# Attention in fp16 on one core: the columns of ones beside the values, written by VectorE and no longer by GpSimd

## The chip, the core and the metric

The kernel runs on one core of a Trainium2 chip. A core has five engines with instruction queues of their own: TensorE (PE in the profile; its weight loads are PEld), VectorE (DVE), ScalarE (ACT), GpSimd (POOL) and SyncE (SP), which here only issues DMAs. Engines wait for each other on semaphores. The metric is the device time of one execution in microseconds; the kernel before has a median of 124.57 us over seven runs.

## The reference

Plain softmax attention over 8 batches of 8 heads, with 512 positions of 64 elements, in float32:

```python
scores = np.einsum('bhqd,bhkd->bhqk', q, k) / np.sqrt(64)
attn = np.exp(scores - scores.max(axis=-1, keepdims=True))
attn = attn / attn.sum(axis=-1, keepdims=True)
out = np.einsum('bhqk,bhkd->bhqd', attn, v)
```

## The kernel before, in words

The 64 heads are worked on in 32 pairs (`NP`), numbered g. A tile of a pair holds both heads: 128 partitions, and 4 rows of 64 elements for each head in each partition.

For a pair, SyncE loads k, q and v (`load`, L318; six buffers for each). GpSimd casts them from float32 to fp16 (`cast_qk`, L331, and `cast_v`, L323). TensorE transposes q and k against an identity matrix (`transposes`, L348), VectorE copies the transposes out of PSUM (`copy`, L355), and TensorE makes the scores transposed, keys in the partitions and queries along the free axis (`scores`, L374). ScalarE takes the exponential of 1024 columns at a time (L379); the maximum is not subtracted. For six of the groups of scores VectorE computes the exponential itself, in seven instructions (L393 to L428). Then TensorE multiplies the exponentials by the values (`values`, L462), and VectorE divides by the sum (`normalise`, L440 and L441). SyncE stores the result (L449).

The sums of the softmax come out of the same matmul as the result. Twelve tiles (`vps`, `NV = 12`) hold the cast values of a pair: for each of the 2 x 4 blocks, 64 columns of values and one more column that holds 1.0. So a value matmul has 65 columns, and the last of them is the sum of the exponentials. The tiles are used in turn, g modulo 12. The columns of ones are written once, before anything else uses the tiles (L608); the casts of v write only the 64 columns beside them. Each write is a memset of 128 partitions and 8 elements, one in every 65.

The order of the work on each engine is fixed when the program is built. The opening is written out by hand: the first loads (`first_loads`, L505 on ScalarE's queue for k and L506 on SyncE's for q, a head at a time), the loads of the next pairs, the identity matrix (`make_identity`, two operations on GpSimd), the ones, and then `first_pair`. In `first_pair` TensorE multiplies a constant by itself (`busy`, L510) until the first q and k are there. VectorE, ScalarE and GpSimd cast parts of the first pair (L520 to L525), TensorE transposes them (L539, L545), VectorE copies them out (L567 to L591), and the first exponentials follow (L557). After the opening the class `Plan` sets the order, with a model of the three busy engines that steps through the kernel 5 ns at a time when the program is built. Nothing in it refers to the ones.

Of the kernel before, what the change touches and what calls it, by code (L numbers as in the profile page):

```python
# [229 lines left out]
def kernel(  # L230
# [7 lines left out]
    nc = tc.nc  # L238
    B, H, S, D = q.shape
# [38 lines left out]
    vps = [cpool.tile([P, 2, NI, D + 1], FP16, name=f"vp{n}") for n in range(NV)]  # L278
# [29 lines left out]
    def load(g, names):  # L308
        if g >= NP:
            return  # L310
        for name in names:
            src = {"q": q, "k": k, "v": v}[name]
            t = load_tile(g, name)
            if name == "v" and g in HALVED:
                for h in range(2):
                    nc.sync.dma_start(out=t[:, h], in_=source(src, g)[:, h])
                continue
            nc.sync.dma_start(out=t[:, :, :, :], in_=source(src, g))  # L318

    def cast_v(g):  # L320
        if g >= NP:
            return
        nc.gpsimd.tensor_copy(out=vps[g % NV][:, :, :, 0:D], in_=raw[g]["v"][:, :, :, :])  # L323

    def cast_qk(g):
        if g >= NP:
            return
        t = qpool.tile([P, 2, NI, P], FP16, tag="qkp", name=f"qkp_{g}")
        for n, name in ((1, "k"), (0, "q")):
            eng = nc.vector if (g, name) == (1, "q") else nc.gpsimd  # L330
            eng.tensor_copy(  # L331
                out=t[:, n].rearrange("p i (h d) -> p h i d", h=2),
                in_=raw[g][name][:, :, :, :],
            )
        qkp[g] = t

    def feed(g):
        load(g + 5, "kqv")
        cast_qk(g + 3)
        cast_v(g + 2)  # L340
# [9 lines left out]
    def copy(g):  # L350
        if g == 1:
            for n in (1, 0):
                nc.vector.tensor_copy(out=tqk[g][:, n], in_=tps[g][:, n].rearrange("p i c -> p (i c)"))  # L353
            return
        nc.vector.tensor_copy(  # L355
            out=tqk[g][:, :, :], in_=tps.pop(g).rearrange("p n i c -> p n (i c)")
        )
# [79 lines left out]
    def normalise(u, n):  # L437
        o, x = os[u // 7], u % 7
        rc = opool.tile([P, 7, 1], FP32, tag="rc", name=f"rc_{u}")
        nc.vector.reciprocal(out=rc[:, 0:n], in_=o[:, x : x + n, D : D + 1])  # L440
        nc.vector.tensor_tensor(  # L441
            out=ring[:, u % NU : u % NU + n, :],
            in0=o[:, x : x + n, 0:D],
            in1=rc[:, 0:n].broadcast_to([P, n, D]),
            op=AluOp.mult,
        )
        while heads and heads[0][2] + NI <= u + n:
            g, h, u0 = heads.pop(0)
            nc.sync.dma_start(  # L449
                out=source(out, g)[:, h], in_=ring[:, u0 % NU : u0 % NU + NI, :]  # L450
            )
# [49 lines left out]
    def first_loads():  # L501
        tk = load_tile(0, "k")
        tq = load_tile(0, "q")
        for h in range(2):
            nc.scalar.dma_start(out=tk[:, h], in_=source(k, 0)[:, h])  # L505
            nc.sync.dma_start(out=tq[:, h], in_=source(q, 0)[:, h])  # L506
# [91 lines left out]
    with tc.manual_schedule():  # L598
        first_loads()
        load(1, "kq")  # L600
        load(0, "v")
        for g in range(2, 5):
            load(g, "kq")
            load(g - 1, "v")
        load(4, "v")
        make_identity(nc, ident)
        for n in range(NV):
            nc.gpsimd.memset(vps[n][:, :, :, D : D + 1], 1.0)  # L608
        first_pair()
        cast_qk(1)  # L610
        cast_v(0)
        cast_qk(2)
        cast_v(1)
        feed(0)
        do = {
            "transposes": transposes,
            "scores": scores,
            "values": values,
            "feed": feed,
            "raise": raise_,  # L620
            "copy": lambda g, b: copy(g),
            "pass": pass_,
            "norm": lambda u, n, b: normalise(u, n),
        }
        for what, *args in Plan(groups, NP, 3).run():
            do[what](*args)
# [30 lines left out]
```

## Time and profile before

| | |
|---|---|
| runs | 124.23, 124.46, 124.47, 124.57, 125.81, 125.82, 125.86 us; median 124.57 |
| the profiled execution | 124.47 us |
| its span, first to last instruction | 122.7 us |
| granted TensorE clock | 0.996 of full speed |
| busy: ScalarE, TensorE, VectorE, GpSimd | 114.3, 108.3, 99.4, 76.5 us |
| the 12 memsets of ones on GpSimd | first start 1.24 us, 138 ns each, 0.53 us together |
| first instruction of VectorE | 3.21 us |

The span is what the profile covers; the execution is 1.77 us longer. Busy time counts an engine's own instructions, not its waits, and the engines work beside each other, so their busy times add up to more than the span. A line of the timeline gives the start, the duration, the engine, the line of the kernel, the operation, and its tiles; the brackets behind it hold how long the engine stood idle before, and what released it.

### The profile page before, as it was taken

The page shows a single profiled execution, that of the slowest core. Times are in us where ns is not written, and L with a number is a line of the kernel's source. Part 1 is how long each engine was busy: PE and PEld are TensorE (multiplying, and loading weights), DVE is VectorE, ACT ScalarE, POOL GpSimd, SP SyncE. Part 2 cuts the span into 40 slices and gives each one's busy share as a digit, 9 for nine tenths or more (in the row PEclk, how much of TensorE's full clock was granted, in tenths as well). Part 3 has the DMA queues.
Part 4 walks back from the last instruction along what each step waited for, and adds up shares of the span by engine and source line. Part 5 has one row for each costly group of instructions (what it writes and reads, how often), then busy time and mean ns, then how long its engine had stood idle before and what let it go on. Part 6 is the DMA issues. An engine that isn't in the chain of part 4 may idle for free.

```text
span 122.7 us, 3967 instructions
## 1 busy us (share of the span) xinstructions
PE 108.3 (88%) x1565; PEld 67.5 (55%) x1565; DVE 99.4 (81%) x159; ACT 114.3 (93%) x127; POOL 76.5 (62%) x113
## 2 busy tenths in 40 slices
PE   7979788989898898998999997989999998899950
PEld 2546445647465465765456573656655665567540
DVE  0546999999989998699999899896979898875260
ACT  4499999999999999999999999999999999999940
POOL 3269799997988579295666958185956679000000
PEclk9999999999999999999999999999999999999998
DMA  3999999999999999995989999997999993131342
GB/s 119 292 352 384 384 377 382 379 353 284 366 352 333 292 331 344 318 330 204 260 275 285 280 308 316 287 305 236 300 293 335 342 326 132 48 115 59 129 138 83
DMA packets 35603, 33.82 MB, mean 276 GB/s; under 512 B 2688, under 2 KB 35584, under 8 KB 35584
## 3 DMA queue, kind: packets, MB, share of 16 engines
q1 hardware_dynamic: 35152, 33.24, 82.8%
q10 hardware_dynamic: 432, 0.33, 0.8%
q8 instruction: 12, 0.20, 0.7%
q14 instruction: 7, 0.06, 0.1%
HBM read 25.17 MB, written 8.39 MB: 273 GB/s over the span
## 4 chain that ended last, share of the span: by engine, by line
ACT 49%; PE 27%; issue 18%; DVE 2%; ACTq 0%
ACT pt L379 49%; PE st L374 10%; PE o L462 8%; PE tp L348 3%; PE st_0a L510 2%; DVE tqk L353 1%; PE st L550 1%; PE o_last L477 1%; DVE ring L441 1%; PE tp_qb L545 0%; DVE obl L490 0%; PE tp_qa L545 0%; PE st L545 0%; PE st_0a L550 0%; DVE kt L591 0%
## 5 line engine op out<-in xcount | busy, mean ns | idle before, releaser
L379 ACT ACTIVATE pt<-st 128x1024 f16<-128x1024 f32 (+1 forms) x120 | 109.4, 1327 | 0.1
L374 PE MATMUL st<-tqk 64*128 64x512 f16 x248 | 48.1, 384 | 7.6 <-ACT pt L379 6.6
L462 PE MATMUL o<-vp,pt 128*128 128x65 f16 x1008 | 46.9, 195 | 1.3 <-ACT pt L379 0.9
L462 PEld LDWEIGHTS <-pt 128*128 128x128 f16 x1008 | 37.1, 98 | 18.4 <-issue 14.7
L331 POOL CAST qkp<-k 128x512 f16<-128x512 f32 x31 | 21.2, 683 | 24.0 <-DMA k<-in_k_dram 15.6
L323 POOL CAST vp<-v 128x512 f16<-128x512 f32 x32 | 29.9, 935 | 0.9 <-DMA v<-in_v_dram 0.8
L331 POOL CAST qkp<-q 128x512 f16<-128x512 f32 x30 | 26.6, 887 | 0.6 <-DMA q<-in_q_dram 0.4
L374 PEld LDWEIGHTS <-tqk 64*128 64x128 f16 x248 | 13.2, 93 | 21.1 <-issue 12.4
L441 DVE TENSOR_TENSOR ring<-o,rc 128x448 f32<-128x448 f32 (+2 forms) x37 | 22.6, 612 | 1.3
L355 DVE COPY tqk<-tp 128x1024 f16<-128x1024 f16 x30 | 20.6, 685 | 2.4 <-PE tp L348 2.1
L348 PE MATMUL tp<-ident,qkp 128*128 128x128 f16 x248 | 19.5, 220 | 0.0
L348 PEld LDWEIGHTS <-qkp 128*128 128x128 f16 x248 | 14.0, 98 | 6.9 <-issue 4.8
L428 DVE SCALAR_TENSOR_TENSOR y<-y,m 128x1024 f32<-128x1024 f32 x12 | 16.4, 1365 | 0.0
L440 DVE RECIPROCAL rc<-o 128x7 f32<-128x7 f32 (+2 forms) x37 | 7.3, 198 | 9.3 <-PE o L462 9.3
L428 DVE SCALAR_TENSOR_TENSOR pt<-y,e 128x1024 f16<-128x1024 f32 x6 | 8.1, 1348 | 0.0
L428 DVE SCALAR_TENSOR_TENSOR y<-m 128x1024 f32<-128x1024 f32 x6 | 8.1, 1346 | 0.0
L393 DVE TENSOR_SCALAR z<-st 128x1024 uint32<-128x1024 f32 x6 | 7.3, 1221 | 0.5 <-PE st L374 0.4
L417 DVE TENSOR_SCALAR e<-z 128x1024 uint32<-128x1024 uint32 x6 | 6.1, 1022 | 0.0
L406 DVE TENSOR_SCALAR m<-z 128x1024 uint32<-128x1024 uint32 x6 | 5.2, 867 | 0.0
L510 PE MATMUL st_0a<-const-bfloat16-1.0 128*128 128x512 bf16 (+1 forms) x8 | 2.9, 548 | 0.8 <-PEq L641 0.8
L510 PEld LDWEIGHTS <-const-bfloat16-1.0 128*128 128x128 bf16 x15 | 1.6, 120 | 2.6 <-issue 2.4
L520 DVE CAST q<-q 128x128 f16<-128x128 f32 x1 | 0.2, 227 | 3.2 <-DMA q<-in_q_dram 3.2
(43 smaller groups left out, 18.9 us busy)
## 6 DMA issues: line engine op xcount, KB each, us to landing
out_dram<-ring SPq DMA_DIRECT2D x63, 128.0 KB, 3.6
k<-in_k_dram SPq DMA_DIRECT2D x31, 256.0 KB, 4.7
q<-in_q_dram SPq DMA_DIRECT2D x31, 256.0 KB, 4.8
v<-in_v_dram SPq DMA_DIRECT2D x27, 256.0 KB, 5.0
v<-in_v_dram SPq DMA_DIRECT2D x10, 128.0 KB, 4.7
k<-in_k_dram ACTq DMA_DIRECT2D x2, 128.0 KB, 2.8
q<-in_q_dram SPq DMA_DIRECT2D x2, 128.0 KB, 2.5
out_dram<-obl SPq DMA_DIRECT2D x1, 64.0 KB, 2.7
```

The source lines that it names most:

```text
L323: nc.gpsimd.tensor_copy(out=vps[g % NV][:, :, :, 0:D], in_=raw[g]["v"][:, :, :, :])
L331: eng.tensor_copy(out=t[:, n].rearrange("p i (h d) -> p h i d", h=2), in_=raw[g][name][:, :, :, :],)
L348: nc.tensor.transpose(tps[g][:, n, i, :], qkp[g][:, n, i, :], ident)
L355: nc.vector.tensor_copy(out=tqk[g][:, :, :], in_=tps.pop(g).rearrange("p n i c -> p n (i c)"))
L374: nc.tensor.matmul(st[:, x, :], kc, qc, start=True, stop=True)
L379: nc.scalar.activation(out=pt[:, 0:size, :], in_=st[:, 0:size, :], func=EXP, scale=scale)
L393: nc.vector.tensor_scalar(out=r["z"][:, :, :], in0=r["st"][:, :, :], scalar1=scale * 1.4426950408889634 * 2.0**23, scalar2=(127 + SHIFT) * ...
L428: nc.vector.scalar_tensor_tensor(out=r["pt"][:, :, :] if n == 3 else r["y"][:, :, :], in0=mant if n == 0 else r["y"][:, :, :], scalar=QUAR ...
L440: nc.vector.reciprocal(out=rc[:, 0:n], in_=o[:, x : x + n, D : D + 1])
L441: nc.vector.tensor_tensor(out=ring[:, u % NU : u % NU + n, :], in0=o[:, x : x + n, 0:D], in1=rc[:, 0:n].broadcast_to([P, n, D]), op=AluOp. ...
L462: nc.tensor.matmul(os[u // 7][:, u % 7, :], blocks[(g, c, h)][:, y * P : (y + 1) * P], vps[g % NV][:, h, c, :], start=(c == 0), stop=(c == ...
L510: nc.tensor.matmul(dst[:, 0:n], ones[:, 0:P], ones[:, 0:n], start=True, stop=True)
```

## The change

One word is different: the twelve memsets are issued on VectorE. In the built program they are VectorE's first twelve instructions, ahead of its cast of the first half of q (L520), and GpSimd goes from the identity matrix straight to its cast of the first half of k (L523). TensorE, ScalarE and SyncE have the same instructions in the same order, and no DMA is different. TensorE waits for VectorE at the same places, with counts that are higher by twelve.

```diff
         make_identity(nc, ident)
         for n in range(NV):
-            nc.gpsimd.memset(vps[n][:, :, :, D : D + 1], 1.0)
+            nc.vector.memset(vps[n][:, :, :, D : D + 1], 1.0)
         first_pair()
         cast_qk(1)
         cast_v(0)
```

## The prediction

> **What bounds the kernel now.** I read the page first: the shares of busy time, then the chain of work that ended last, then the costliest groups. ScalarE is busy for 93% of the span, more than any other engine, and its exponentials hold half of the chain:
>
> ```profile
> PE 108.3 (88%) x1565; PEld 67.5 (55%) x1565; DVE 99.4 (81%) x159; ACT 114.3 (93%) x127; POOL 76.5 (62%) x113
> ...
> ACT 49%; PE 27%; issue 18%; DVE 2%; ACTq 0%
> ...
> L379 ACT ACTIVATE pt<-st 128x1024 f16<-128x1024 f32 (+1 forms) x120 | 109.4, 1327 | 0.1
> ```
>
> The reader is to see the last number: 0.1 us of idle time ahead of 120 exponentials. From its first exponential on, ScalarE never stops, so a delay of that first one moves the end by about its own length, and nothing else in the opening counts.
>
> The change touches only the opening, so the next view is the timeline of the first microseconds, VectorE and GpSimd side by side. Columns: start, duration, engine, line and operation, tiles, and in brackets the idle time before and what ended it.
>
> ```profile
> 1.01 0.29 POOL masks.py:199 TENSOR_SCALAR_AFFINE_SELECT ident<-ident 128x128 f16<-128x128 f16 x1
> 1.24 0.53 POOL L608 MEMSET vp<- 128x8 f16 x12
> ...
> 3.21 0.30 ACT L522 CAST q<-q 128x128 f16<-128x128 f32 x1 [0.27 <-DMA q<-in_q_dram]
> 3.21 0.23 DVE L520 CAST q<-q 128x128 f16<-128x128 f32 x1 [3.21 <-DMA q<-in_q_dram]
> ...
> 3.38 0.23 DVE L521 CAST k<-k 128x128 f16<-128x128 f32 x1
> 3.41 0.35 POOL L523 CAST k<-k 128x128 f16<-128x128 f32 x1 [1.64 <-DMA k<-in_k_dram]
> ```
>
> Two things are to be seen. GpSimd writes the ones at 1.24 to 1.77 us and then stands idle for 1.64 us, until the first half of k lands. VectorE does nothing at all until 3.21 us, when the first half of q lands; ScalarE's cast of the same load starts at the same 3.21, so the load, and not an engine, sets that moment.
>
> The chain of waits in order of time shows what the opening costs the end:
>
> ```profile
> 0.73 0.04 issue
> 0.77 2.93 PE st_0a L510 x8
> 3.71 0.35 PE tp_qa L545 x4
> 4.06 0.22 PE st_ka L539
> ```
>
> TensorE's placeholder matmuls fill 0.77 to 3.71 us; the transposes of q and k follow. Neither the ones nor GpSimd stand in it.
>
> **The change part by part.**
>
> *Taken from GpSimd: 12 memsets.* They hold its queue from 1.24 to 1.77 us, 0.53 us together (138 ns each, started about 35 ns apart). Behind them stands the cast of k at L523, which waits for its load until 3.41 in any case. VectorE's cast of k waits for the same load and starts at 3.38, so all that an earlier GpSimd could win is 0.03 us, and I take nothing. Ahead of the memsets stand only the two operations on the identity matrix (end 1.30); they do not move. No DMA is issued by GpSimd or by the moved lines; SyncE's loads stand in another queue and are not passed by anything.
>
> *Added to VectorE: the same 12 memsets, as its first instructions.* The listing of the built program shows them ahead of the cast at L520, waiting for nothing but the start of the program. TensorE's and GpSimd's first work is at 0.74 and 0.73 us, so I let VectorE begin at 0.74. It has until 3.21: 2.47 us of cover, or 0.206 us for each of the 12.
>
> The trace shows no VectorE memset, so its price is bounded. From below: the same shape on GpSimd, one per 0.035 us, 0.4 us in all. From above: the whole duration of the smallest VectorE cast here, 128 columns, 0.227 us, with no overlap between neighbours: 12 x 0.227 = 2.72 us, end at 3.46, that is 0.25 us late. The nearest rows are VectorE's own. L520 and L521 start 0.17 us apart though each lasts 0.23, so neighbours overlap. A cast of 512 columns (L331) takes 0.42 us and one of 128 takes 0.227: (420 - 227) / 384 = 0.5 ns a column. Eight columns in place of 128 save 0.06 us, which leaves 0.11 us from start to start. I take 0.11: 12 x 0.11 = 1.3 us, finished at about 2.1 us, 1.1 us ahead of the load. Cost on the path: nothing. The cover is the wait for q; if q landed at 1.0 us instead, about 1 us of the 1.3 would be on the path.
>
> The Trainium skill speaks to this price in "VectorE: DVE Perf Modes", section "The TRN2 errata — SBUF-src ops pay a fixed extra latency per instruction", where the measured fixed part of one operation is put at about 150 cycles of 0.96 GHz. An estimate from that page is 12 x 158 / 0.96 = 1.98 us, finished at 2.7 us, and the sum would again be nothing.
>
> *The ports.* While VectorE writes the ones, GpSimd builds the identity (0.73 to 1.30 us), which it did alone before. Suppose that the two shut each other out altogether. Then the identity is late by at most VectorE's whole stretch, 1.3 us by my price, and ready by 2.6; TensorE first reads it at 3.64 us. By the upper bound (2.72 us) it is ready at 4.02, 0.38 us late. The trace shows that the two engines can hold each other up elsewhere: the cast of v on GpSimd takes 0.61 us at its shortest and 1.61 at its longest, the latter beside a long VectorE operation. In the opening I take nothing for it.
>
> The Trainium skill states in "SBUF — State Buffer", section "Who interferes with whom", that a VectorE instruction outside its two-port modes and with at most one SBUF input does not contend with GpSimd, while copies and casts in those modes lock GpSimd out for the whole instruction. A memset has no input; by the first half of the rule the sum is nothing, by the second it is the delay of the identity that the sentences above bound.
>
> *Waits.* None is added. The listing shows the same waits on every engine, only with other counts: TensorE's first transposes wait for VectorE's thirteenth instruction where it was the first. That wait ends when the cast at L520 ends, as before. The value matmuls (L462) still wait for GpSimd's cast of v alone, because the ones are already covered by TensorE's wait for that first cast. The casts of v into the same tiles, first at 7.61 us, get no wait on VectorE.
>
> *Everything after 3.7 us* has the same instructions in the same order on all five queues. VectorE's 1.3 us more of work does not matter to its later share, since it falls into idle time.
>
> **Sum.** The profiled execution took 124.47 us, its span 122.7, so 1.77 lies around it. 122.7 + 0 + 1.77 = 124.47; the bounds of the priced parts are -0.03 and +0.38. The median of the seven runs is 124.57, 0.1 above the profiled one. I forecast 124.5.
>
> **The rivals.**
>
> *The ones come late (slower).* Place: VectorE's queue ahead of L520. It decides from 0.206 us a memset; beyond it the cast of q, the first transposes and every exponential are late by 12 x (c - 0.206). For over 1% (1.25 us) a memset would need 0.31 us; at 0.35 us it is 1.73 us and 126.2. For it: no VectorE memset is in the trace, and the first instruction of an engine may be dearer than its neighbours. Against it: no VectorE row of this trace, down to 4 columns (0.175 us) and up to 128 (0.227), is that dear, and it would have to be so for eight columns with no input.
>
> *The same work, but a later group of runs.* Of the seven runs of the kernel before, four lie at 124.23 to 124.57 and three at 125.81 to 125.86. The profile is of the lower group and doesn't show what sets the upper one apart. Nothing in the edit favours either, but a median of a few runs can fall there: 124.47 + 1.35 = 125.8, which is +1.0%.
>
> *A start worth something (faster).* GpSimd reaches L523 0.5 us sooner. Against it: its idle time there ends on the load, and the gain is at most the 0.03 us worked out above: 124.44. A time over 1% lower would need 123.3, below every run shown, and I find no term for it.
>
> *The edit does nothing at all*, because the order of instructions is not what the source says. The listing of the built program excludes it: 12 memsets leave GpSimd's queue and 12 stand at the head of VectorE's. Were it so, the time would be the same 124.5.
>
> **How the numbers follow.** One per cent, 1.25 us, is about what a measurement of this kernel can tell from no change. Forecast, nothing on the path: 0.82, counting in the 0.03 us gain and the doing-nothing case, which give the same time. Upper group: 0.13, half of it just over 1%. Late ones: 0.02 over 1%. Something unseen: 0.03, faster by over 1%. So faster 0.03, same 0.82 + 0.065 = 0.885, rounded to 0.88, slower 0.065 + 0.02 = 0.085, rounded up to 0.09. The range starts at 124.0: the lowest run, 124.23, less the 0.03, less half the lower group's width of 0.34. It ends at 125.9, the top of the upper group; the +0.38 of the bounds lies within it.
>
> **What would show it.** In the profile after: VectorE's memsets from about 0.74 us, at 0.11 us from start to start, done before 3.21; its cast at L520 still ended by q's load at about 3.2; GpSimd idle from 1.3 us to about 3.4; the identity done by about 1.3; the first exponential at about 5.43; ScalarE's 120 exponentials with about 0.1 us of idle time before them. I am wrong if L520 is ended by something else than its load, if the identity is finished after 3.6 us, or if ScalarE shows idle time that it doesn't show now.

## The result

The changed kernel is faster: a median of 123.59 us over 27 runs against 124.70 us over 64 runs of the kernel before; the ratio is 0.9916, with a 95% interval of 0.9897 to 0.9935. That is about 1.05 us, 0.8 to 1.3. The prediction, 124.5 us with a range of 124.0 to 125.9, is too high, and its range does not hold the result.

The runs of every kernel here fall into two groups about 1.4 us apart, in shares that vary and that the ratios count unequally, so the fairer comparison is of the runs within 1.2 us of a kernel's fastest: a median of 123.53 us after against 124.45 before, 0.92 us less.

The opening went as forecast. From the timeline of the changed kernel, start, duration, engine, line:

```profile
0.83 0.46 DVE L608 MEMSET vp<- 128x8 f16 x12 [0.83 <-PEq L641]
1.01 0.29 POOL masks.py:199 TENSOR_SCALAR_AFFINE_SELECT ident<-ident 128x128 f16<-128x128 f16 x1
...
3.29 0.23 DVE L520 CAST q<-q 128x128 f16<-128x128 f32 x1 [2.00 <-DMA q<-in_q_dram]
3.29 0.30 ACT L522 CAST q<-q 128x128 f16<-128x128 f32 x1 [0.36 <-DMA q<-in_q_dram]
...
3.46 0.23 DVE L521 CAST k<-k 128x128 f16<-128x128 f32 x1
3.49 0.34 POOL L523 CAST k<-k 128x128 f16<-128x128 f32 x1 [2.19 <-DMA k<-in_k_dram]
```

VectorE writes the ones in 0.46 us and then waits two more microseconds for q. GpSimd waits 2.19 us for k where it waited 1.64. Nothing starts earlier for it; the casts even start 0.08 us later, with their loads.

The page of the changed kernel shows the same bound, and the last of these lines differs from its counterpart before:

```profile
ACT 54%; PE 22%; issue 19%; DVE 2%; ACTq 0%
...
L379 ACT ACTIVATE pt<-st 128x1024 f16<-128x1024 f32 (+1 forms) x120 | 109.4, 1327 | 0.1
...
out_dram<-obl SPq DMA_DIRECT2D x1, 64.0 KB, 1.8
```

In the page of the kernel before, the same line of the DMA issues reads:

```profile
out_dram<-obl SPq DMA_DIRECT2D x1, 64.0 KB, 2.7
```

ScalarE's 120 exponentials take 109.4 us with 0.1 us of idle time, as before. But the last store, half of the last head, on SyncE's queue, lands 1.8 us after its issue and no longer 2.7. The end of the program waits for it.

So the two profiled executions, 124.47 and 123.26 us with spans of 122.7 and 121.5, part in two places. The last multiplication (L490) ends at 118.36 + 0.42 = 118.78 us (118.79 before rounding) instead of 118.69 + 0.42 = 119.11: 0.33 us. From there to the end of the span it takes 2.69 us instead of 3.58: 0.88 us before rounding. The line of L490 in the timeline of the changed kernel (that of the kernel before stands further down):

```profile
118.36 0.42 DVE L490 TENSOR_TENSOR obl<-o_last,rc_last 128x256 f32<-128x256 f32 x1
```

### The profile page after: what moved, and what is told of

Its sections match the earlier page's. It is cut to its first block, busy times and chain, and to the rows that moved or that the text cites. A ratio compares the mean times of both kernels' runs of the same rounds, so it can differ in the third digit from the quotient of the medians.

```text
span 121.5 us, 3967 instructions
## 1 busy us (share of the span) xinstructions
PE 107.6 (89%) x1565; PEld 67.1 (55%) x1565; DVE 97.3 (80%) x171; ACT 114.3 (94%) x127; POOL 73.3 (60%) x101
## 4 chain that ended last, share of the span: by engine, by line
ACT 54%; PE 22%; issue 19%; DVE 2%; ACTq 0%
ACT pt L379 54%; PE st L374 8%; PE o L462 6%; PE tp L348 3%; PE st_0a L510 2%; DVE tqk L353 1%; PE st L550 1%; PE o_last L477 1%; DVE ring L441 1%; DVE obl L490 0%; PE tp_qa L545 0%; PE tp_qb L545 0%; PE st L545 0%; DVE kt L591 0%; PE st L510 0%
## 5 line engine op out<-in xcount | busy, mean ns | idle before, releaser
L379 ACT ACTIVATE pt<-st 128x1024 f16<-128x1024 f32 (+1 forms) x120 | 109.4, 1327 | 0.1
L331 POOL CAST qkp<-k 128x512 f16<-128x512 f32 x31 | 26.3, 850 | 23.1 <-DMA k<-in_k_dram 13.8
L323 POOL CAST vp<-v 128x512 f16<-128x512 f32 x32 | 25.8, 808 | 0.9 <-DMA v<-in_v_dram 0.8
L331 POOL CAST qkp<-q 128x512 f16<-128x512 f32 x30 | 22.5, 750 | 3.5 <-DMA q<-in_q_dram 3.1
L428 DVE SCALAR_TENSOR_TENSOR y<-y,m 128x1024 f32<-128x1024 f32 x12 | 15.2, 1262 | 0.0
L406 DVE TENSOR_SCALAR m<-z 128x1024 uint32<-128x1024 uint32 x6 | 4.3, 720 | 0.0
```

Of the source, the lines that this page charges most:

```text
L331: eng.tensor_copy(out=t[:, n].rearrange("p i (h d) -> p h i d", h=2), in_=raw[g][name][:, :, :, :],)
L379: nc.scalar.activation(out=pt[:, 0:size, :], in_=st[:, 0:size, :], func=EXP, scale=scale)
L428: nc.vector.scalar_tensor_tensor(out=r["pt"][:, :, :] if n == 3 else r["y"][:, :, :], in0=mant if n == 0 else r["y"][:, :, :], scalar=QUAR ...
```

## Where the 0.88 us at the end came from

SyncE's waits in the last microseconds (L652 is the wait for all stores at the end of the program), each line with the total, how often and the longest, first of the kernel before, then of the changed one:

```profile
SPq L652 <- DMA out_dram<-obl: 1.3, 2, 1.0
SPq L652 <- DMA out_dram<-ring: 0.7, 2, 0.5
```

```profile
SPq L652 <- DMA out_dram<-ring: 0.7, 2, 0.4
...
SPq L652 <- DMA out_dram<-obl: 0.3, 1, 0.3
```

The wait for the last store shrank from 1.3 to 0.3 us, and the other did not change. The DMA view of the kernel before, from 120.4 to 121.2 us in 40 slices of 20 ns, shows what was in the way: busy tenths of the 16 DMA engines, GB/s, and the queues that moved something.

```profile
DMA  9989494321000000000000000000000000000000
GB/s 282 257 256 257 128 563 128 103 52 26 0 0 0 0 0 0 0 0 0 0 0 0 0 0 0 0 26 26 26 26 0 0 0 0 0 0 0 0 0 0
...
q14 instruction: 1, 0.01, 3.3%
```

At 120.6 us almost everything has been sent. Then nothing starts for 0.3 us, and four slices around 120.95 bring the rest. The queue named instruction moved one packet of 8 KB in this window. The trace's records of single packets place it: it starts at 120.50 us and takes 0.43. The last five packets of the last store start from 120.93 to 121.02, directly behind it, one after another. Fifteen of the sixteen parts of that store had landed by 121.05; the sixteenth landed at 121.85. I read this as one DMA engine that fetched instructions while its share of the last store stood in line; the records do not name the engine of a packet. The fetch explains about 0.4 us of the lateness (the packet before the gap starts at 120.62, the last one at 121.02). The other 0.4 us lies between the last packet and its landing, and no run here says why.

The DMA view from 118 to 121.5 us has all of the last stores. In the kernel before it has the fetch, and the two halves of the last head, issued within 0.01 us of each other, take 2.7 and 1.7 us to land:

```profile
q14 instruction: 1, 0.01, 0.8%
...
out_dram<-obl SPq DMA_DIRECT2D x1, 64.0 KB, 2.7
out_dram<-obl ACTq DMA_DIRECT2D x1, 64.0 KB, 1.7
```

In the changed kernel the same stretch has two queues and no instruction queue:

```profile
q1 hardware_dynamic: 576, 0.46, 40.7%
q10 hardware_dynamic: 144, 0.07, 6.5%
```

There the packet is found at 113.30 us, in the window from 112.8 to 114.5:

```profile
q14 instruction: 1, 0.01, 1.3%
```

This gives a theory. **Theory A**: some engine's next 8 KB of program is fetched by the DMA engines that also move the data; the engine is VectorE, and the fetch starts when VectorE comes near a fixed place in its program. Twelve instructions more at the head bring VectorE to that place 12 instructions sooner, and the fetch starts 5.5 us before the last store is issued (113.30 against 118.82) instead of in the middle of it. The rivals: **B**, GpSimd's relief; **C**, a gain that grows with the work moved; **D**, VectorE's early start in itself.

## The experiments

Every kernel keeps the lines of the kernel before. "Tail" is the stretch from the end of the last multiplication (L490) to the end of the span. "Fetch" is the start of the last 8 KB instruction packet, relative to the end of L490 (the two times are behind it). Instructions of VectorE are counted in the built program, waits among them; each trace holds two fewer. The ratios are to runs of the kernel before, for the experiments on the same chip. The last column is the median of the runs within 1.2 us of the kernel's fastest, less the same median of the kernel before that the ratio is taken to.

| kernel | VectorE's instructions | fetch, us | tail, us | ratio, 95% interval | near the fastest, us |
|---|---|---|---|---|---|
| before | 196 | +1.39 (120.50, 119.11) | 3.58 | | |
| the change | 208 | -5.49 (113.30, 118.79) | 2.69 | 0.9916, 0.9897 to 0.9935 | -0.92 |
| spare memsets at the start | 208 | -5.50 (113.66, 119.16) | 2.71 | 0.9945, 0.9911 to 0.9979 | -0.86 |
| one of twelve | 197 | +0.06 (118.94, 118.88) | 3.14 | 0.9996, 0.9961 to 1.0032 | -0.53 |
| spare memsets at the end | 208 | +0.06 (118.98, 118.92) | 3.22 | 0.9988, 0.9943 to 1.0032 | -0.23 |
| one wide memset | 196 | +1.43 (121.99, 120.56) | 3.63 | 1.0069, 1.0026 to 1.0112 | +0.16 |
| four of twelve | 200 | -0.39 (120.07, 120.46) | 3.30 | 0.9969, 0.9923 to 1.0015 | -0.41 |
| two of twelve | 198 | +0.18 (119.27, 119.09) | 3.31 | 0.9961, 0.9921 to 1.0001 | -0.35 |
| one less | 195 | +3.34 (122.26, 118.92) | 3.00 | 0.9955, 0.9911 to 0.9998 | -0.86 |
| two less | 194 | +3.46 (122.53, 119.07) | 2.81 | 0.9909, 0.9876 to 0.9943 | -0.81 |
| change, fetch put back | 196 | +1.44 (121.91, 120.47) | 3.62 | 1.0017, 0.9976 to 1.0058 | +0.03 |
| change again | 208 | -5.54 (113.57, 119.11) | 2.70 | 0.9952, 0.9906 to 0.9998 | -0.81 |

The intervals are wide beside 0.9 us (0.7%). The last column has 7 to 21 runs of a kernel; it follows the change of the tail within 0.3 us in every row, while the tail and the fetch are read from one profile each.

One more thing is the same in all of these profiles. Each store lands in sixteen parts. Where the fetch starts between 0.4 us before and 1.5 us after the end of L490, one part of the last store lands 0.25 to 0.88 us behind the last of the other fifteen. In the kernels with the fetch elsewhere, no last part is more than 0.05 us behind, in any of the last five stores.

**Spare memsets at the start.** The ones stay on GpSimd, and VectorE writes a tile that nobody reads.

```diff
-            nc.gpsimd.memset(vps[n][:, :, :, D : D + 1], 1.0)
+            nc.gpsimd.memset(vps[n][:, :, :, D : D + 1], 1.0); nc.vector.memset(spare[:, n, :], 1.0)
```

> The ones stay on GpSimd; VectorE gets 12 memsets of a spare tile that nobody reads, as its first instructions. Theory A, the fetch at the end: the gain comes from VectorE's program being 12 instructions longer ahead of its last ones, which brings its last 8 KB instruction fetch some 7 us forward, out of the way of the last store. It expects the same gain as the change, about -0.9 us (ratio about 0.993), and a last store on SyncE's queue that lands about 1.8 us after its issue where it took 2.7. Theory B, GpSimd's relief: the gain is from GpSimd no longer writing the ones. It expects no difference (ratio 1.000), the landing at 2.7 us.

The fetch moved to 113.66 us, the tail fell to 2.71 us, the last store on SyncE's queue lands 1.8 us after its issue, and the ratio is 0.9945. GpSimd has exactly its old program here, so theory B falls: its relief is not needed for the gain.

**One of twelve.** Only the first of the 12 memsets moves to VectorE.

```diff
-            nc.gpsimd.memset(vps[n][:, :, :, D : D + 1], 1.0)
+            (nc.vector if n < 1 else nc.gpsimd).memset(vps[n][:, :, :, D : D + 1], 1.0)
```

> One of the 12 memsets on VectorE, 11 on GpSimd. Theory A: the fetch comes one VectorE instruction earlier, about 119.7 us in place of 120.5, ahead of most of the last store's packets; most of the gain, -0.5 to -0.9 us (ratio 0.993 to 0.996). Theory B, or any in which the gain grows with the work that is moved: a twelfth of the gain, -0.08 us (ratio 0.999).

A single instruction of 65 ns moved the fetch by 1.3 us against the end of L490 and took 0.44 us off the tail. The profiled execution took 123.83 us. The ratio, 0.9996, misses the expectation and cannot tell this from nothing; the last column has -0.53 us, in line with the tail and at the lower end of what I expected. The fetch came at 118.94 us and not at 119.7: early enough to spare the last store in part (its late part lands at 121.18, 0.45 us behind the others), but not to miss the stores in front of it, of which three have one part that lands 0.3 to 0.7 us behind.

**Spare memsets at the end.** Twelve memsets of the spare tile behind L490.

```diff
-        )
+        ); [nc.vector.memset(spare[:, n, :], 1.0) for n in range(NV)]
```

> The ones stay on GpSimd; the 12 spare memsets stand at the end of VectorE's program, behind the last multiplication (L490). Theory A: VectorE reaches the place that starts the fetch at the same point of its work as before, so the fetch still falls into the last store: no gain (ratio 0.998 to 1.002), landing 2.7 us after the issue. A theory in which the mere number of VectorE's instructions counts, wherever they stand, expects about -0.9 us (ratio 0.993).

Here theory A, as I had put it, missed. I expected the fetch to stay 1.4 us after L490; it came at +0.06 us, as with one of twelve. The tail is 3.22 us, between the two cases; the ratio is 1 within its interval, and the last column has -0.23 us. What stands behind L490 does matter. In the kernel before that is a drain, an instruction that lasts until L490 is finished (118.70 to 119.17 us, L490 to 119.11); here it is memsets, which do not wait (the first starts at 118.88, L490 ends at 118.92). This suggests, and does not show, that in the kernel before the place that starts the fetch lies at or behind that drain, and that VectorE's queue reaches it when the instruction in front lets go. A theory by which only the number of VectorE's instructions counts is not met either: the number is that of the change, and the tail is not.

**One wide memset.** The twelve tiles are one, and GpSimd writes all the ones with one instruction.

```diff
-    vps = [cpool.tile([P, 2, NI, D + 1], FP16, name=f"vp{n}") for n in range(NV)]
+    vall = cpool.tile([P, NV, 2, NI, D + 1], FP16, name="vp"); vps = [vall[:, n] for n in range(NV)]
...
-        for n in range(NV):
-            nc.gpsimd.memset(vps[n][:, :, :, D : D + 1], 1.0)
+        for n in range(1):
+            nc.gpsimd.memset(vall[:, :, :, :, D : D + 1], 1.0)
```

> The ones stay on GpSimd but are written by one memset of all 12 tiles, which are one tile here; GpSimd's program is 11 instructions shorter, VectorE's is as before. Theory A: no gain (ratio 0.998 to 1.002), since VectorE's fetch stays where it was. Theory B in the form that GpSimd's shorter queue is what helps: about -0.9 us (ratio 0.993).

GpSimd's program is 11 instructions shorter and nothing is gained: fetch at +1.43, tail 3.63. Together with the spare memsets this rules GpSimd out, as the engine that gains and as the one whose fetch it is. The ratio, 1.0069, is above my expectation, and by its interval the kernel would be slower; but the last column has only +0.16 us and the tail is 0.05 us longer. Whether the 0.16 us is anything but scatter, no run settles.

**Four of twelve, and two of twelve.** As one of twelve, with `n < 4` and `n < 2`.

> Four of the 12 memsets on VectorE, eight on GpSimd. Theory A (the place of VectorE's last 8 KB instruction fetch): the fetch falls at about 117.5 to 118.3 us, clear of the last store; from the end of the last multiplication (L490) to the end of the span 2.7 to 2.9 us, where it was 3.58 before and 2.69 after the change; gain -0.7 to -0.9 us (ratio 0.993 to 0.995). Theory C (the gain grows with the work moved): a third, -0.3 us (ratio 0.998).

> Two of the 12 on VectorE. Theory A: the fetch at 118.3 to 118.9 us, the stretch from L490 to the end between 2.7 and 3.1 us, gain -0.4 to -0.9 us, more than with one and no more than with four. Theory C: a sixth, -0.15 us.

Both gave less than half of the gain by the last column (-0.41 and -0.35 us; both ratios, 0.9969 and 0.9961, have 1 in their intervals), and my sizes were wrong. With two the fetch came behind the end of L490 and not before it, the tail is 3.31 us where I expected 3.1 at most, and the gain is not above that with one. With four I expected the fetch clear of the stores, 0.8 us or more before the end of L490, and it came 0.39 us before it. In its profile the stores in front are hit instead: one part of sixteen of each of two earlier stores lands 1.0 and 0.8 us behind the other parts, SyncE's issue of the next store takes 0.97 us (the one before it 0.42), and so SyncE issues its half of the last store only at 121.05 us, 0.56 us after ScalarE issues the other half. Theory C is not met: one, two, four and twelve memsets gave tails of 3.14, 3.31, 3.30 and 2.69 us. The full gain comes somewhere between four and twelve.

**One less, and two less.** The ones stay on GpSimd, and VectorE loses one or two casts of the opening to engines that cast the other half of the same tile anyway. SyncE's program loses one wait for a load with them (L318).

```diff
-        nc.vector.tensor_copy(out=q16[:, 0, 0:2], in_=tq[:, 0, 0:2])     # two less
-        nc.vector.tensor_copy(out=k16[:, 0, 0:2], in_=tk[:, 0, 0:2])     # one less, two less
-        nc.scalar.copy(q16[:, 0, 2:4], tq[:, 0, 2:4])                    # two less
-        nc.gpsimd.tensor_copy(out=k16[:, 0, 2:4], in_=tk[:, 0, 2:4])     # one less, two less
+        nc.scalar.copy(q16[:, 0, 0:4], tq[:, 0, 0:4])                    # two less
+        nc.gpsimd.tensor_copy(out=k16[:, 0, 0:4], in_=tk[:, 0, 0:4])     # one less, two less
```

> The opposite direction: the ones stay on GpSimd, and VectorE gets one instruction less, because GpSimd casts the first half of k in one instruction of 256 columns (L523) and VectorE's L521 is gone. Theory A: the fetch is put off by one instruction of VectorE, past the last wait of its program; if it falls behind the last store the stretch from L490 to the end is about 2.7 us and the gain about -0.9 us; if the fetch starts while VectorE stands at that wait, it stays near 120.5 and there is no gain. Theory D (VectorE's early memsets help in themselves) and theory C expect no gain in either case, and the fetch has no part in them.

> As the kernel with one less, and ScalarE casts the first half of q in one instruction of 256 columns (L522) so that VectorE's L520 is gone too: two instructions less on VectorE. The cast of q takes 0.41 us in place of 0.23, which may cost the opening up to 0.2 us. Theory A: the fetch falls behind the last store, or out of the span; the stretch from L490 to the end is 2.7 us, gain -0.7 to -0.9 us. Theories C and D: no gain, or a loss of up to 0.2 us.

This is the test in the opposite direction, and it came out for theory A: with less on VectorE the kernel is faster too, 0.9955 and 0.9909 (-0.86 and -0.81 us). The DMA view of the kernel with one less, from 121.5 to 123 us, shows a single packet. It is the fetch, behind the last store, which landed 1.8 us after its issue:

```profile
DMA packets 1, 0.01 MB, mean 5 GB/s; under 512 B 0, under 2 KB 0, under 8 KB 0
...
q14 instruction: 1, 0.01, 2.2%
```

The tail is 3.00 us and not 2.7. In this kernel VectorE's next instruction of the closing barrier starts 0.48 us after the one in front of it (121.09 to 121.57), where the kernel before shows 0.12 (122.16 to 122.28); 0.36 us is lost there, and the profile does not say to what.

**The change, with the fetch put back.** The ones on VectorE as in the change, and 12 instructions less in the middle of its program: 11 reciprocals and a wait. TensorE's program loses four waits with them.

```diff
-        rc = opool.tile([P, 7, 1], FP32, tag="rc", name=f"rc_{u}")
-        nc.vector.reciprocal(out=rc[:, 0:n], in_=o[:, x : x + n, D : D + 1])
+        rc = keep if u == 7 or u in range(70, 147) else opool.tile([P, 7, 1], FP32, tag="rc", name=f"rc_{u}")
+        None if u in range(70, 147) else nc.vector.reciprocal(out=rc[:, 0:n], in_=o[:, x : x + n, D : D + 1])
```

> The change as it is, ones on VectorE, but with 12 instructions less in the middle of VectorE's program: 11 of the reciprocals (L440, between units 70 and 146) are left out and the sums of an earlier group are used in their place, and one wait goes with them. So 77 of the 256 blocks of the result are divided by sums that aren't theirs, and VectorE has about 2.2 us less to do, in a stretch that ScalarE bounds. VectorE's program is as long as before the change, with the same last instructions. Theory A: the last 8 KB instruction fetch falls into the last store again (about 1.4 us after the end of L490), the stretch from L490 to the end is about 3.6 us, and the gain of the change is gone: ratio to the kernel before 0.998 to 1.001. Theory D (the early memsets on VectorE, or GpSimd's relief, help in themselves): the gain stays or grows with the work left out: -0.9 us or more, ratio 0.993 or below.

> The change itself on the same chip, beside the kernel with the fetch put back. Theory A: fetch at about 113 us, the stretch from L490 to the end 2.7 us, gain about -0.9 us (ratio 0.991 to 0.994). The opening is expected to differ from run to run and not between the kernels: the first exponential at 5.2 to 5.5 us, earlier where TensorE's clock is granted earlier.

The gain is gone: ratio 1.0017, last column +0.03 us, fetch at +1.44 us, tail 3.62, although the memsets stand where the change put them and VectorE has less to do. Theory D falls with it. From the page of this kernel, the last store:

```profile
out_dram<-obl SPq DMA_DIRECT2D x1, 64.0 KB, 2.8
```

The change itself, run again beside it, gave 0.9952, a little less than the 0.991 to 0.994 expected, and -0.81 us in the last column. Its profile happens to have the same opening as the one of the kernel before. The last lines of the timeline, first before, then the change again:

```profile
118.69 0.42 DVE L490 TENSOR_TENSOR obl<-o_last,rc_last 128x256 f32<-128x256 f32 x1
119.14 0.39 SPq L497 DMA_DIRECT2D out_dram<-obl  x1
```

```profile
118.69 0.42 DVE L490 TENSOR_TENSOR obl<-o_last,rc_last 128x256 f32<-128x256 f32 x1
119.14 0.39 SPq L497 DMA_DIRECT2D out_dram<-obl  x1
```

After 119 us both kernels are at the same hundredth of a microsecond. Yet one execution took 124.47 us and the other 123.59: all of the 0.88 us lies behind these lines.

## The 0.33 us of the opening

They are not the change's. TensorE runs its first matmuls at half speed, and the moment at which the full clock comes differs from execution to execution. In the timelines the eight transposes of the first q (L545) tell it, before, after, and in the change again:

```profile
4.43 0.63 PE L545 MATMUL tp_qb<-ident,q 128*64 128x128 f16 x8
```

```profile
4.50 0.41 PE L545 MATMUL tp_qb<-ident,q 128*64 128x128 f16 x8
```

```profile
4.43 0.64 PE L545 MATMUL tp_qb<-ident,q 128*64 128x128 f16 x8
```

By the trace's record of the clock, full speed begins at 5.63, 4.40 and 5.63 us; the first exponential (L557) starts at 5.43, 5.17 and 5.43. The difference of the first two is 0.26 us there, 0.32 from the third exponential on and 0.33 at the end of L490. The first and the third are different kernels and alike; the second and the third are the same kernel and differ.

The clock can also come much later. In the profiles of the wide memset, of four of twelve and of the fetch put back, full speed begins at 9.88 to 10.07 us, and L490 ends at 120.46 to 120.56 us; in the nine others full speed begins at 4.35 to 5.63 us, and L490 ends at 118.79 to 119.16, some 1.4 us sooner. The Trainium skill, in "TensorE: Matmul & The Clock Gate", section "What's actually happening", says that the gate watches windows of about 3.4 us that run freely and do not start with the kernel; these profiles agree: full speed lasts 116.05 us in the nine and 112.64 us in the three, which is 3.41 us less, and begins at another moment in almost every one.

## Why the prediction was wrong

*What bounds the kernel*: right. ScalarE's 120 exponentials take the same 109.4 us with 0.1 us before them, and the 0.32 us by which the third exponential came sooner in the profile after arrived at L490 as 0.33 us.

*Taken from GpSimd, nothing*: right. Its wait before the cast at L523 still ends on the load, and neither a wide memset nor the old memsets beside spare ones moved the time by way of GpSimd.

*Added to VectorE, hidden*: right in kind; the size was 0.036 us from start to start and not 0.11. It is the price of the same memset on GpSimd (0.035), the lower bound. All twelve took 0.46 us, so the prediction's other estimate, 1.98 us, is four times too long for this memset. They end at 1.29 us, two microseconds ahead of the load. The identity is finished at 1.30 us as before, so the ports cost nothing.

*Waits*: right. VectorE's first cast is released by the load of q as before.

*"Everything after 3.7 us has the same instructions in the same order on all five queues"*: this is the step that failed. The sentence is true, and the conclusion that nothing changes there does not follow, because the same instructions stand at other places in VectorE's program, and with them the fetch stands at another time. The sum put nothing for the end of the span. I took the 3.58 us between L490 and the end of the span over unchanged, with the 1.77 us outside the span; the 1.77 us held (123.26 against a span of 121.5), and the 3.58 us became 2.69. So the term that I had at 0 was -0.88 us. The DMA view of the kernel before had it in sight: the last store on SyncE's queue took 2.7 us to land and its twin on ScalarE's queue 1.7, and a queue called instruction had seven packets. I had followed neither to the end of the span.

*The rivals.* For "faster" I wrote that I found no term; there was one, outside the opening. "Late ones" was far off, at 0.036 us against 0.206. "A later group" did not happen: the median after is below the fastest of the 64 runs before, 123.95 us. The sum of the working was 124.47; with the right tail it is 124.47 - 0.88 = 123.59, the time of the profile of the change again, which has the opening of the kernel before. That it is also the median to the hundredth is luck.

The Trainium skill says in "Runtime: NRT & Kernel Launch", section "Instruction fetch mechanics", that a sequencer fetches the next block of its program by its own DMA queue while it executes the present one, and calls the cost of a block's boundary mostly hidden. Ahead of the end ScalarE agrees with that: in the kernel before six such packets fall between 34 and 108 us, and it shows 0.1 us of idle time before its 120 exponentials. At the end the fetch is not hidden: with 0.43 us of fetching in front of it, one part of the last store landed 0.8 us late. The section gives blocks of 16 KiB; here the packets of this queue are of 8 KB.

What stays open: which rule fixes the place in VectorE's program, what sets the time from there to the fetch, and why the late part lands 0.8 us late when its packets are 0.4 us late. What happens between four and twelve memsets was not resolved further. Whether another queue or another split of the last store would dodge the fetch was not tried. No version here is faster than the change beyond the measurement: the spare memsets (0.9945), one and two casts less (0.9955, 0.9909) reach the same time in another way.

## What to carry to other kernels

Follow the end of the span down to the landing of the last store, and compare twins: two equal transfers issued together that land a microsecond apart, as the 2.7 and 1.7 us here, may have something in the way. An edit that adds or removes instructions on an engine can shift that engine's instruction fetches in time, as it did for VectorE here, even if everything it does is hidden; look where the last fetch falls against the last stores, and if it falls among them, a few instructions more or less ahead of it are worth trying. Before a small difference of two profiles is given to an edit, check that the granted clock came at the same moment in both.

## What was not expected of the hardware

A VectorE memset of 128 x 8 elements costs 0.036 us from start to start when 12 follow each other (65 ns each by itself), no more than on GpSimd, where the profile shows 138 ns each and 0.035 us from start to start. One 8 KB instruction fetch of 0.43 us went with a 64 KB store that landed 0.8 us late: fifteen of its sixteen parts were done, and the end waits for the last. And the kernel got faster by one instruction less on an engine (ratio 0.9955) as well as by twelve more (0.9916).
